# Queueing every weight load from the second paired block on in the order in which its buffer comes free

## The chip, the cores and the metric

The kernel runs on one core of a Trainium2 chip. The metric is the device time of one execution in microseconds; the median of three runs of the kernel before is 1049.4 us (1048.66 to 1050.55). A core has five engines that the text names: PE (TensorE, matrix products), DVE (VectorE), ACT (ScalarE), POOL (GpSimd) and SP (SyncE, which here only issues DMAs). Each has its own list of instructions, in the order in which the kernel wrote them, and they meet through semaphores. In the rows of SP a load whose buffer is not free holds back the loads written behind it.

## What is computed

One layer of a hybrid encoder on 256 rows of width 2048: a differential-attention group and a convolution group side by side, an output projection, then a gated feed-forward network. The part that matters here is the last:

```python
h = h + jnp.einsum('bsm,md->bsd', mixed, w_out[l].astype(mixed.dtype))
hn = rms_norm(h, norm2_g[l])
a = jnp.einsum('bsd,df->bsf', hn, w_gate[l].astype(hn.dtype))
bu = jnp.einsum('bsd,df->bsf', hn, w_up[l].astype(hn.dtype))
h = h + jnp.einsum('bsf,fd->bsd', jax.nn.silu(a) * bu, w_down[l].astype(hn.dtype))
```

w_gate and w_up are 2048 x 5632, w_down is 5632 x 2048, all float32. Every weight is read from device memory once.

## The kernel before

**Products in parts.** A float32 product is made of products in a shorter float format. Each weight tile W is split into a rounded part hi and the rest lo = W - hi, each activation likewise, and PE adds three products: hi by hi, lo activation by hi weight, hi activation by lo weight.

**Chunks.** The program is a list of chunks, each a piece of a weight matrix with its load, its *round* (hi), its *split* (lo) and its *multiply*. There are two kinds.

A *plain* chunk is two slices of 128 rows by 512 columns. `load_chunk` (L305) asks for a buffer `raw`, of which there are `RAW_BUFS` = 5, and has SP load 512 KB into it (L315). `round_chunk` (L318) has ACT make `whi` (L320). For most chunks `split_chunk` (L326) has DVE subtract (L329, `wlo`). For some, marked `by_dma`, ACT writes -raw into `wlo` (L323) and POOL issues a DMA that adds raw to it (L324); this text calls it the accumulate. PE's products are L1014 and L1015 (with hi) and L1020 (with lo). A raw buffer comes free when DVE's split, or the accumulate, has read it.

A *pair* chunk (`kind` "s") takes two slices each of w_gate and w_up (or of two column blocks of w_down) and forms seven combined weights, so that seven products do the work of eight. `load_pair` (L952) has SP load two times 512 KB into a buffer `wb` (L956), of which there are 2; `round_pair` and `split_pair` (L959, L971) use DVE (L966 to L968, L975, L976) and ACT (L969, L972). A pair's buffer comes free with DVE's L975. PE's products are L993 to L995.

**Blocks.** The first 512 columns of the hidden layer (block 0) are plain. Each later block is a paired block: four plain chunks of w_gate, four of w_up and four pairs. The order of its chunks is `FIRST_ORDER` for the first paired block, "gsggsgsuusuu", and `ORDER`, "sggsggsuusuu", for the others (L84, L85). This text writes g1 to g4, u1 to u4 and s1 to s4 for the chunks of the first paired block, and G1, S1 and so on for those of the one after it. Its chunks u2 and u4 are `by_dma`, and so are G1, G2, U2 and U4 of the second. After 4, 4 and 3 blocks comes a pass over w_down of the same two kinds of chunk.

**What sets the order.** `run_chunks` (L387) walks over the chunks. At chunk t it writes down, in this order, splits up to t + 2, pair loads up to t + `PAIR_AHEAD` = t + 6, then for each chunk up to t + 3 its load and its round, more splits, and then the products of chunk t. A pair of the first paired block is not loaded more than three chunks ahead; from the second block on (`behind`, L390) pairs are loaded up to six ahead while plain chunks are loaded three ahead. So a pair's two loads stand in SP's queue ahead of plain loads that are used earlier.

After a block's last product with w_gate, ACT copies a sum out of PE's accumulators (L1092), DVE adds six more (L1094 to L1099), ACT applies SiLU (L1105), and DVE finishes the block (L1113, L1115). These stand on ACT's and DVE's queues between the rounds and splits of the next block's first chunks.

Of the kernel before, what the change touches and what calls it, by code (L numbers as in the profile page):

```python
# [63 lines left out]
RAW_BUFS = 5  # L64
# [14 lines left out]
NS = 4  # L79
# [16 lines left out]

HI_AHEAD, LO_AHEAD = 3, 2

PAIR_AHEAD = 6

FIRSTS = [sum(FGROUPS[: g + 1]) for g in range(len(FGROUPS))]

# [20 lines left out]
def tile_block(  # L123
# [120 lines left out]
    def resume():  # L244
        chunks_done[0] += 1
        for g in list(running):
            if next(g, StopIteration) is StopIteration:
                running.remove(g)
# [14 lines left out]
    side = []  # L263
# [21 lines left out]
    chunks = []  # L285
    before = {}
# [99 lines left out]

    def run_chunks():  # L387
        n = len(chunks)
        i = j = p = 0
        behind = [k for k in range(n) if chunks[k].get("kind") == "s"][NS]  # L390
        for t in range(n):
            hi_lead, lo_lead = lead(t)
            while j < min(i, t + 1 + lo_lead):
                chunks[j]["split"](chunks[j])
                j += 1
            while p < min(n, t + 1 + PAIR_AHEAD):
                if chunks[p].get("kind") == "s":

                    if p < behind and p > t + hi_lead:
                        break  # L400
                    load_pair(chunks[p])
                p += 1
            while i < min(n, t + 1 + hi_lead):
                if i in before:
                    before[i]()
                chunks[i]["load"](chunks[i])
                chunks[i]["round"](chunks[i])
                i += 1
                if hi_lead == lo_lead:
                    chunks[j]["split"](chunks[j])  # L410
                    j += 1
            while j < min(n, t + 1 + lo_lead):
                chunks[j]["split"](chunks[j])
                j += 1
            chunks[t]["multiply"](chunks[t])
            if chunks[t].get("prompt") and chunks[t]["done"]:
                resume()
        while running:
            resume()
# [532 lines left out]
    def load_pair(c):  # L952
        c["b"] = early.tile([P, 4, N], F32, tag="wb", name="wb")
        for i, kind in enumerate("ug"):
            w, col = c["from"][kind]
            sp.dma_start(out=c["b"][:, 2 * i : 2 * i + 2, :],  # L956
                         in_=w.rearrange("(k p) n -> p k n", p=P)[:, c["rows"], col : col + N])
# [82 lines left out]
    def fast_block(order, pairs, twos, sources, operands, half, whole, by_dma=dict(g=(), u=())):  # L1040

        units, sums = [], {}
        left = dict(s=list(pairs), g=list(twos), u=list(twos))
        for kind in order:
            what = left[kind].pop(0)
            c = dict(kind=kind, sums=sums, done=None, first={}, last={}, rows=what["rows"], **operands)
            if kind == "s":
                c.update(p=what["p"], load=lambda c: None, round=round_pair, split=split_pair, multiply=multiply_pair,
                         uses=[q for q, _, _ in PRODUCTS])
                c["from"] = sources  # L1050
            else:
                w, col = sources[kind]
                c.update(ks=what["ks"], w=w, nk=2, width=N, cols=[(col, N)], by_dma=what["k"] in by_dma[kind],
                         load=load_chunk, round=round_chunk, split=split_chunk, multiply=multiply_two,
                         uses=(Q3, QX) if kind == "u" else (Q2, Q4))
            units.append(c)
        assert not any(left.values())
        for q in range(8):
            users = [c for c in units if q in c["uses"]]
            users[0]["first"][q] = users[-1]["last"][q] = True  # L1060
        [c for c in units if c["kind"] != "u"][-1]["done"] = half
        units[-1].update(done=whole, prompt=True)
        chunks.extend(units)

    def gate_up_block(j):
        fast_block(ORDER if j > 1 else FIRST_ORDER, [dict(p=p, rows=slice(p, p + HK + 1, HK)) for p in range(NS)],
                   [dict(ks=ks, rows=slice(ks[0], ks[1] + 1, ks[1] - ks[0]), k=ks) for ks in TWOS],
                   dict(g=(w_gate, j * N), u=(w_up, j * N)),
                   dict(pairs=lambda: forms.get("pair"), plain=lambda k: forms["plain"][k]),
                   products_done, lambda sums: block_done(j, sums),  # L1070
                   BY_DMA if j > 1 and j not in FIRSTS else dict(g=(), u=BY_DMA["u"]))

    def down_pass(g, j0, nb):
        k0 = j0 * HD
        ks = [k for k in range(nb * HD) if k >= 2 * HD or k % HD >= ND]
        twos = [dict(ks=(k0 + a, k0 + b), rows=slice(k0 + a, k0 + b + 1, b - a), k=None)
                for a, b in zip(ks[::2], ks[1::2])]
        for i, order in enumerate(DORDERS[nb]):
            n = 2 * i
            end = {}  # L1080
            fast_block(order, [dict(p=p, rows=slice(k0 + p, k0 + p + HD + 1, HD)) for p in range(ND)], twos,
                       dict(g=(w_down, n * N), u=(w_down, (n + 1) * N)),
                       dict(pairs=lambda: down_forms.get(g), plain=actT.get),
                       lambda sums, n=n, end=end: down_half(g, n, sums, end),
                       lambda sums, n=n, end=end: down_whole(g, n, sums, end))
# [130 lines left out]
    before[OPENING] = lambda: start(late_constants())  # L1216
    before[XWHOLE] = x_whole
    run_chunks()


# [26 lines left out]
```

## Time and profile before

| what | value |
|---|---|
| median of three runs | 1049.4 us |
| profiled execution | 1048.92 us, span 1047.1 us |
| PE busy | 1036.2 us (99%) |
| DVE, ACT, POOL busy | 900.6, 621.6, 100.5 us |
| granted clock | 1.000 |
| loads by SP (queue q1) | 203.71 MB, 56.9% of the 16 DMA engines' span |
| DMAs by POOL (queue q0) | 26.74 MB, 13.4% |

The paired blocks begin at about 383 us of the span. A row of the order of time gives start, duration, engine, line, operation, what it writes and reads, how many it merges, and in brackets how long the engine idled before it and what ended that. SP's rows are the moments of issue; the time from issue to landing stands in the view of DMAs. Names of tiles are the kernel's: raw and wb are the loaded weights, whi and wlo the two parts, wt, wh, wlb and wlt those of a pair, q the accumulators.

### The profile page before, as it was taken

The numbers are of one execution on the slowest core, as the hardware profiler recorded it, in microseconds if no ns is written. First come the engines' busy times: TensorE is split into PE (matmuls) and PEld (weight loads), VectorE is DVE, ScalarE is ACT, GpSimd is POOL, SyncE is SP. The second block draws the span as 40 slices with busy tenths as digits, with TensorE's granted clock in tenths as the row PEclk, the third lists the DMA queues.
The fourth block names the chain that finished last, engine by engine and source line by source line (L and its number), as shares of the span: only waits on it lengthen the run. The fifth ranks groups of instructions, "written<-read, shape, count | busy, mean of one in ns | idle before, by whom it ended". The sixth has DMA issues, their size and how long they took to land.

```text
span 1047.1 us, 12933 instructions
## 1 busy us (share of the span) xinstructions
PE 1036.2 (99%) x4663; PEld 852.5 (81%) x4663; DVE 900.6 (86%) x1095; ACT 621.6 (59%) x786; POOL 100.5 (10%) x143
## 2 busy tenths in 40 slices
PE   9999999999999999999999999999999999999998
PEld 7888887877788788888888888888888888888886
DVE  7899889898765599999787898999878789989897
ACT  7544666755756565776463657666644446657442
POOL 0130122201100100000001010000000110000010
PEclk9999999999999999999999999999999999999999
DMA  9657654453546566987867789879757879798683
GB/s 335 227 182 280 212 163 167 154 181 134 177 153 226 194 223 214 268 266 236 232 210 188 217 271 273 256 217 285 248 175 241 219 208 291 222 287 267 187 265 85
DMA packets 113936, 231.30 MB, mean 221 GB/s; under 512 B 7504, under 2 KB 8656, under 8 KB 113616
## 3 DMA queue, kind: packets, MB, share of 16 engines
q1 hardware_dynamic: 104864, 203.71, 56.9%
q0 software_dynamic: 8864, 26.74, 13.4%
q8 instruction: 36, 0.59, 0.2%
q14 instruction: 28, 0.23, 0.1%
q10 hardware_dynamic: 144, 0.03, 0.0%
HBM read 204.24 MB, written 9.44 MB: 204 GB/s over the span
## 4 chain that ended last, share of the span: by engine, by line
PE 61%; DMA 2%; DVE 2%; issue 1%; ACT 0%; DVEq 0%; POOLq 0%
PE q L1020 12%; PE q L1014 12%; PE q L1015 12%; PE q L995 8%; PE q L993 7%; PE q L994 7%; DMA raw<-in_w_down_dram 1%; PE ps_a L831 1%; DMA wlo<-raw 1%; PE acc L365 1%; PE acc L359 1%; PE acc L360 1%; DVE wlo L329 1%; DVE wlt L976 0%; DVE wt L966 0%
## 5 line engine op out<-in xcount | busy, mean ns | idle before, releaser
L320 ACT CAST whi<-raw 128x1024 fp32r<-128x1024 f32 (+1 forms) x273 | 281.5, 1048 | 141.6 <-PE acc L360 58.9
L329 DVE TENSOR_TENSOR wlo<-raw,whi 128x1024 fp32r<-128x1024 f32 (+1 forms) x239 | 287.8, 1218 | 73.5 <-ACT whi L320 73.3
L972 ACT CAST wh<-wt 128x2048 fp32r<-128x2048 f32 x52 | 99.6, 1914 | 77.6 <-DVE wt L968 76.9
L976 DVE TENSOR_TENSOR wlt<-wt,wh 128x2048 fp32r<-128x2048 f32 x52 | 119.1, 2290 | 14.9 <-ACT wh L972 14.7
L359 PE MATMUL acc<-whi,xhi 128*128 128x512 f32 x320 | 126.9, 397 | 1.0 <-ACT whi L320 0.9
L360 PE MATMUL acc<-whi,xlo 128*128 128x512 f32 x320 | 125.2, 391 | 0.0
L1014 PE MATMUL q<-whi,chi 128*128 128x512 f32 x320 | 125.2, 391 | 0.0
L1015 PE MATMUL q<-whi,clo 128*128 128x512 f32 x320 | 124.5, 389 | 0.0
L993 PE MATMUL q<-wh,fhi 128*128 128x512 f32 x280 | 109.9, 393 | 0.0
L994 PE MATMUL q<-wh,flo 128*128 128x512 f32 x280 | 109.1, 390 | 0.0
L517 DVE SCALAR_TENSOR_TENSOR y<-upad,cw,y 128x256 f32<-128x256 f32 x240 | 102.2, 482 | 2.2 <-ACT y L510 2.2
L1014 PE MATMUL q<-whi,ahi 128*128 128x512 f32 x256 | 100.2, 391 | 0.0
L1015 PE MATMUL q<-whi,alo 128*128 128x512 f32 x256 | 99.6, 389 | 0.0
L975 DVE TENSOR_TENSOR wlb<-wb,wh 128x1536 fp32r<-128x1536 f32 x52 | 91.1, 1752 | 1.8 <-ACT wh L969 1.8
L365 PE MATMUL acc<-wlo,xhi 128*128 128x512 f32 x320 | 87.8, 396 | 2.0 <-DVE wlo L329 2.0
L1020 PE MATMUL q<-wlo,chi 128*128 128x512 f32 x320 | 85.7, 390 | 0.2 <-DMA wlo<-raw 0.2
L969 ACT CAST wh<-wb 128x1536 fp32r<-128x1536 f32 x52 | 76.6, 1474 | 0.0
L365 PEld LDWEIGHTS acc<-wlo,xhi 128*128 128x128 f32 x320 | 59.7, 189 | 15.3 <-DVE wlo L329 3.3
L359 PEld LDWEIGHTS acc<-whi,xhi 128*128 128x128 f32 x320 | 60.4, 189 | 14.3 <-ACT whi L320 1.9
L1020 PEld LDWEIGHTS q<-wlo,chi 128*128 128x128 f32 x320 | 59.9, 188 | 13.2 <-DMA wlo<-raw 0.8
L360 PEld LDWEIGHTS acc<-whi,xlo 128*128 128x128 f32 x320 | 60.4, 189 | 12.2
L1014 PEld LDWEIGHTS q<-whi,chi 128*128 128x128 f32 x320 | 60.1, 188 | 12.3
(230 smaller groups left out, 1739.1 us busy)
## 6 DMA issues: line engine op xcount, KB each, us to landing
raw<-in_w_in_dram SPq DMA_DIRECT2D x79, 512.0 KB, 4.6
raw<-in_w_down_dram SPq DMA_DIRECT2D x64, 512.0 KB, 7.2
raw<-in_w_gate_dram SPq DMA_DIRECT2D x48, 512.0 KB, 7.5
raw<-in_w_up_dram SPq DMA_DIRECT2D x48, 512.0 KB, 6.2
wb<-in_w_up_dram SPq DMA_DIRECT2D x40, 512.0 KB, 3.7
wb<-in_w_gate_dram SPq DMA_DIRECT2D x40, 512.0 KB, 4.9
wlo<-raw POOLq DMA_DIRECT2D x34, 512.0 KB, 7.1
raw<-in_w_out_dram SPq DMA_DIRECT2D x32, 512.0 KB, 4.2
```

The source lines that it names most:

```text
L320: act.copy(c["hi"], c["raw"])
L329: dve.tensor_tensor(c["lo"], c["raw"], c["hi"].bitcast(F32), ALU.subtract)
L359: pe.matmul(ps[m], xhi[:, ms], hi[:, j, :], start=c["first"] and j == 0, stop=False)
L360: pe.matmul(ps[m], xlo[:, ms], hi[:, j, :], start=False, stop=False)
L365: pe.matmul(ps[m], xhi[:, ms], lo[:, j, :], start=False, stop=c["last"] and j == nk - 1)
L517: dve.scalar_tensor_tensor(y[:, ct, :], src, wk, y[:, ct, :], ALU.mult, ALU.add)
L976: dve.tensor_tensor(lot, c["t"], c["hi"][:, :SUMMED].bitcast(F32), ALU.subtract)
L993: pe.matmul(ps, hi, c["hi"][:, w], start=bool(first), stop=False)
L994: pe.matmul(ps, lo, c["hi"][:, w], start=False, stop=False)
L1014: pe.matmul(ps, xs[i][0][:, ms], hi[:, i, :], start=i == 0 and bool(c["first"].get(qs[m])), stop=False)
L1015: pe.matmul(ps, xs[i][1][:, ms], hi[:, i, :], start=False, stop=False)
L1020: pe.matmul(sum_bank(c, qs[m]), xs[i][0][:, ms], lo[:, i, :], start=False, stop=i == 1 and bool(c["last"].get(qs[m])))
```

## The change

`PAIR_AHEAD` goes. From the second paired block on, loads are no longer tied to a distance in chunks. Two lists, `ahead`, hold the plain chunks and the pairs that are not loaded yet, from the second paired block to the end. `freed` says which chunk held the buffer that the head of a list will get (five places back among the plain chunks, two among the pairs), and whether that chunk's split has been written down; for a `by_dma` chunk the walk must have reached it. `load_freed` then queues the loads whose buffer comes free, the earlier chunk's first. It is called twice at each chunk, as soon as the walk is near the first paired block's chunks (`t + hi_lead >= behind - NS`). The first paired block's own loads are still written down when the walk is three chunks away, and a pair's now at the place of its chunk.

```diff
--- before.py
+++ after.py
@@ -96,7 +96,7 @@
 
 HI_AHEAD, LO_AHEAD = 3, 2
 
-PAIR_AHEAD = 6
+PAIR_BUFS = 2
 
 FIRSTS = [sum(FGROUPS[: g + 1]) for g in range(len(FGROUPS))]
 
@@ -386,32 +386,62 @@
 
     def run_chunks():
         n = len(chunks)
-        i = j = p = 0
-        behind = [k for k in range(n) if chunks[k].get("kind") == "s"][NS]
+        i = j = 0
+        pairs = [k for k in range(n) if chunks[k].get("kind") == "s"]
+        raws = [k for k in range(n) if chunks[k].get("kind") != "s" and not chunks[k].get("spare_raw")]
+        behind = pairs[NS]
+        loaded, split = set(), set()
+
+        def load(k):
+            if k not in loaded:
+                loaded.add(k)
+                if k in before:
+                    before[k]()
+                chunks[k]["load" if chunks[k].get("kind") != "s" else "fetch"](chunks[k])
+
+        def split_next():
+            chunks[j]["split"](chunks[j])
+            split.add(j)
+
+        ahead = [[which[a] for a in range(len(which)) if which[a] >= behind] for which in (raws, pairs)]
+        place = [{k: a for a, k in enumerate(which)} for which in (raws, pairs)]
+
+        def freed(side, t):
+
+            if not ahead[side]:
+                return None
+            k = (raws, pairs)[side][place[side][ahead[side][0]] - (RAW_BUFS, PAIR_BUFS)[side]]
+            return k if k in split and (t >= k or not chunks[k]["by_dma"]) else None
+
+        def load_freed(t):
+            while True:
+                ready = [(k, side) for side in range(2) if (k := freed(side, t)) is not None]
+                if not ready:
+                    return
+                load(ahead[min(ready)[1]].pop(0))
+
         for t in range(n):
             hi_lead, lo_lead = lead(t)
             while j < min(i, t + 1 + lo_lead):
-                chunks[j]["split"](chunks[j])
+                split_next()
                 j += 1
-            while p < min(n, t + 1 + PAIR_AHEAD):
-                if chunks[p].get("kind") == "s":
-
-                    if p < behind and p > t + hi_lead:
-                        break
-                    load_pair(chunks[p])
-                p += 1
+            if t + hi_lead >= behind - NS:
+                load_freed(t)
             while i < min(n, t + 1 + hi_lead):
-                if i in before:
-                    before[i]()
-                chunks[i]["load"](chunks[i])
+                load(i)
+                for which in ahead:
+                    if i in which:
+                        which.remove(i)
                 chunks[i]["round"](chunks[i])
                 i += 1
                 if hi_lead == lo_lead:
-                    chunks[j]["split"](chunks[j])
+                    split_next()
                     j += 1
             while j < min(n, t + 1 + lo_lead):
-                chunks[j]["split"](chunks[j])
+                split_next()
                 j += 1
+            if t + hi_lead >= behind - NS:
+                load_freed(t)
             chunks[t]["multiply"](chunks[t])
             if chunks[t].get("prompt") and chunks[t]["done"]:
                 resume()
@@ -1045,7 +1075,7 @@
             what = left[kind].pop(0)
             c = dict(kind=kind, sums=sums, done=None, first={}, last={}, rows=what["rows"], **operands)
             if kind == "s":
-                c.update(p=what["p"], load=lambda c: None, round=round_pair, split=split_pair, multiply=multiply_pair,
+                c.update(p=what["p"], fetch=load_pair, by_dma=False, round=round_pair, split=split_pair, multiply=multiply_pair,
                          uses=[q for q, _, _ in PRODUCTS])
                 c["from"] = sources
             else:
```

The instructions of PE, DVE, ACT and POOL stand in the same order before and after. Only SP's queue changes. The first place is the joint between the first and the second paired block, on SP, before. wb_3906 is s4, wb_3909 S1 and wb_3982 S2 (each in two loads); raw_3859, raw_3887, raw_3944 and raw_3963 are u1 to u4, raw_4017 and raw_4049 G1 and G2. What a row waits for stands in brackets by engine or DMA counter.

```order
L315 DMA raw_3859<-in_w_up_dram 128x2x512 [waits DMAHW7_49]
L315 DMA raw_3887<-in_w_up_dram 128x2x512 [waits DMAHW0_49]
L956 DMA wb_3906<-in_w_up_dram 128x2x512 [waits DMAHW2_49,DMAHW3_49,DMAHW1_49,DVE_49]
L956 DMA wb_3906<-in_w_gate_dram 128x2x512
L956 DMA wb_3909<-in_w_up_dram 128x2x512 [waits DMAHW6_49,DMAHW5_49,DVE_49]
L956 DMA wb_3909<-in_w_gate_dram 128x2x512 [waits DMAHW4_49]
L315 DMA raw_3944<-in_w_up_dram 128x2x512
L315 DMA raw_3963<-in_w_up_dram 128x2x512
L956 DMA wb_3982<-in_w_up_dram 128x2x512 [waits DMAHW2_49,DMAHW7_49,DMAHW1_49,DVE_49]
L956 DMA wb_3982<-in_w_gate_dram 128x2x512 [waits DMAHW0_49]
L315 DMA raw_4017<-in_w_gate_dram 128x2x512
L315 DMA raw_4049<-in_w_gate_dram 128x2x512
```

The same place after. wb_3889 is S1, wb_3913 s4, wb_3948 S2; raw_3892 is G2, raw_3894 u2, raw_3951 u3, raw_3970 and raw_3972 G3 and G4, raw_3974 u4. G1 (raw_3887) stands just ahead of the first row.

```order
L986 DMA wb_3889<-in_w_up_dram 128x2x512 [waits DMAHW2_49,DMAHW3_49,DMAHW1_49,DVE_49]
L986 DMA wb_3889<-in_w_gate_dram 128x2x512
L315 DMA raw_3892<-in_w_gate_dram 128x2x512
L315 DMA raw_3894<-in_w_up_dram 128x2x512 [waits DMAHW4_49]
L986 DMA wb_3913<-in_w_up_dram 128x2x512 [waits DMAHW6_49,DMAHW5_49,DVE_49]
L986 DMA wb_3913<-in_w_gate_dram 128x2x512
L986 DMA wb_3948<-in_w_up_dram 128x2x512 [waits DMAHW6_49,DMAHW7_49,DMAHW5_49,DVE_49]
L986 DMA wb_3948<-in_w_gate_dram 128x2x512 [waits DMAHW0_49]
L315 DMA raw_3951<-in_w_up_dram 128x2x512 [waits DMAHW1_49]
L315 DMA raw_3970<-in_w_gate_dram 128x2x512 [waits DMAHW2_49]
L315 DMA raw_3972<-in_w_gate_dram 128x2x512 [waits DMAHW4_49,DMAHW3_49,DMASW0_49]
L315 DMA raw_3974<-in_w_up_dram 128x2x512 [waits DMAHW1_49,DVE_49]
```

S1 has moved ahead of s4, S2 ahead of u3, and G1 to G4 ahead of u4; u4's load now waits for DVE.

On ACT nothing moved. This is its order at the same place after, which the steps of the prediction follow: u3, u4 with the accumulate's first half, S1, G1, the sums of the first paired block, G2.

```order
L320 CAST whi_3953<-raw_3951 128x1024 [waits DMAHW1_49,PE_49,Activation_49]
L320 CAST whi_3976<-raw_3974 128x1024 [waits DMAHW4_49,PE_49,Activation_49]
L323 ACTIVATE wlo_3978<-raw_3974 128x1024 [waits PE_49]
L999 CAST wh_3994<-wb_3889 128x1536 [waits DMAHW2_49]
L1002 CAST wh_3994<-wt_3993 128x2048 [waits DVE_49]
L320 CAST whi_4028<-raw_3887 128x1024 [waits DMAHW0_49,PE_49,Activation_49]
L323 ACTIVATE wlo_4030<-raw_3887 128x1024 [waits DMASW0_49,PE_49]
L1122 COPY sum0_4041<-q0_3791 128x512 [waits PE_49]
L1135 ACTIVATE sum0_4041<-sum0_4041 128x512 [waits DVE_49]
L1135 ACTIVATE sum2_4043<-sum2_4043 128x512 [waits DVE_49]
L320 CAST whi_4060<-raw_3892 128x1024 [waits DMAHW3_49,PE_49,Activation_49]
L323 ACTIVATE wlo_4062<-raw_3892 128x1024 [waits PE_49]
```

The rows show that everything of the next block on ACT stands behind u3's and u4's rounds.

The second place is a later block (the second of the second group), on SP, before. wb_5613 is its pair S2, wb_5703 S3; the raw rows are G1 to G4.

```order
L956 DMA wb_5613<-in_w_up_dram 128x2x512 [waits DMAHW7_49,DMAHW0_49,DVE_49]
L956 DMA wb_5613<-in_w_gate_dram 128x2x512
L315 DMA raw_5648<-in_w_gate_dram 128x2x512 [waits DMAHW1_49]
L315 DMA raw_5680<-in_w_gate_dram 128x2x512 [waits DMAHW2_49]
L956 DMA wb_5703<-in_w_up_dram 128x2x512 [waits DMAHW4_49,DMAHW3_49,DVE_49]
L956 DMA wb_5703<-in_w_gate_dram 128x2x512
L315 DMA raw_5752<-in_w_gate_dram 128x2x512 [waits DMAHW5_49,DMASW2_49]
L315 DMA raw_5770<-in_w_gate_dram 128x2x512 [waits DMAHW6_49]
```

The same block after; wb_5513 is S1 and wb_5583 S2.

```order
L315 DMA raw_5479<-in_w_gate_dram 128x2x512 [waits DMAHW5_49,DVE_49]
L986 DMA wb_5513<-in_w_up_dram 128x2x512 [waits DMAHW7_49,DMAHW6_49,DVE_49]
L986 DMA wb_5513<-in_w_gate_dram 128x2x512
L315 DMA raw_5532<-in_w_gate_dram 128x2x512 [waits DMAHW0_49,DVE_49]
L986 DMA wb_5583<-in_w_up_dram 128x2x512 [waits DMAHW2_49,DMAHW3_49,DMAHW1_49,DVE_49]
L986 DMA wb_5583<-in_w_gate_dram 128x2x512
L315 DMA raw_5603<-in_w_gate_dram 128x2x512 [waits DMASW2_49]
L315 DMA raw_5605<-in_w_gate_dram 128x2x512 [waits DMAHW4_49,DVE_49]
```

The pairs no longer run ahead: G1 now stands before S1 and G2 before S2, where before S2 stood ahead of both.

## The prediction

> **What bounds the kernel now.** I read the shares of the engines first, then tables of windows, then who waits for whom, and last the order of time around the joint of the first two paired blocks. The page:
>
> ```profile
> PE 1036.2 (99%) x4663; PEld 852.5 (81%) x4663; DVE 900.6 (86%) x1095; ACT 621.6 (59%) x786; POOL 100.5 (10%) x143
> ```
>
> TensorE is the bound. The change acts from 383 us on, where the paired blocks begin, so the table of windows is cut there (columns: window, its length, PE busy with its matmuls, granted clock, share of the DMA engines, GB/s):
>
> ```profile
> 383.00:1005.00 622.00, 621.60 (x2780) 1.00 0.79 238
> 1005.00:1047.10 42.10, 37.87 (x165) 1.00 0.60 174
> ```
>
> In 622 us PE idles 0.4 us; in the last 42 us it idles 4.2, most of it the output's tail. So no order of loads can win more than 4.6 us, and hardly more than 0.6. The clock is full throughout.
>
> [...]
>
> The waits from 383 us on (who waited, for whom: total us, times, longest):
>
> ```profile
> SPq L956 <- DVE wlb L975: 336.4, 41, 13.4
> SPq L315 <- DVE wlo L329: 131.0, 49, 11.2
> ACT whi L320 <- DMA raw<-in_w_down_dram: 22.7, 5, 7.7
> PE q L1020 <- DMA wlo<-raw: 0.2, 1, 0.2
> ```
>
> SP's queue of loads really stands behind pair loads (L956) that wait for a buffer, and ScalarE does wait for plain loads behind them. But PE, which uses a chunk three chunks after it is loaded, lost 0.2 us by it. The waits that the change can remove are covered already. What it can add has no such cover, so I looked for loads that are queued later.
>
> **The change, part by part.** PE, DVE, ACT and POOL keep their order; SP has the same loads in another one. No instruction is added to the four; where the new order of issue needs more separate waits on SP, they stand in front of loads that would wait anyway, so I cost them at nothing.
>
> *In the second and later paired blocks* plain loads go ahead of the pair loads that were queued up to six chunks early. The nearest price of what this frees is the 22.7 us of ACT above, which lay under PE's work: 0 to 0.6 us gained, and I take 0.2.
>
> *At the joint of the first and second paired block* the order shows three loads of the first block put behind loads of the second: pair s4 behind S1; plain u3 behind S2; plain u4 behind G3 and G4. u4 also gets no buffer of its own: of the five, G1, G2, G3 and G4 (all used after u4) hold four and u3 the fifth, so its wait on DVE is one for the split of u3. This is SP before (x2 is two loads):
>
> ```profile
> 402.15 0.37 SPq L956 DMA_DIRECT2D wb<-in_w_up_dram  x1
> 410.15 0.37 SPq L956 DMA_DIRECT2D wb<-in_w_up_dram  x1
> 410.56 0.47 SPq L956 DMA_DIRECT2D wb<-in_w_gate_dram  x1
> 411.07 0.98 SPq L315 DMA_DIRECT2D raw<-in_w_up_dram  x2
> 418.74 0.37 SPq L956 DMA_DIRECT2D wb<-in_w_up_dram  x1
> 419.75 0.98 SPq L315 DMA_DIRECT2D raw<-in_w_gate_dram  x2
> ```
>
> 402.15 is s4, 410.15 S1, 411.07 u3 and u4, 418.74 S2, each pair load the moment its buffer is split. Times from issue to landing, in this order: the second half of the pair at 410.56; the plain load at 411.07; a plain load behind a pair with no accumulate running (393.03, and the shortest, 853.13); two plain loads alone (978 to 985); the accumulates (wlo<-raw) from 383 to 980, min/median/max; the one issued at 436.97.
>
> ```profile
> wb<-in_w_gate_dram SPq DMA_DIRECT2D x1, 512.0 KB, 4.5
> raw<-in_w_up_dram SPq DMA_DIRECT2D x1, 512.0 KB, 7.4
> raw<-in_w_up_dram SPq DMA_DIRECT2D x1, 512.0 KB, 6.1
> raw<-in_w_gate_dram SPq DMA_DIRECT2D x1, 512.0 KB, 5.4
> raw<-in_w_down_dram SPq DMA_DIRECT2D x2, 512.0 KB, 3.5
> DMA to landing us min/median/max: 5.0/7.1/10.2
> DMA to landing us min/median/max: 5.6/5.6/5.6
> ```
>
> The engines that use these loads, before, VectorE first, then ScalarE, POOL and PE:
>
> ```profile
> 414.38 1.22 DVE L966 TENSOR_TENSOR wt<-wb 128x1024 f32<-128x1024 f32 x1
> 416.96 1.75 DVE L975 TENSOR_TENSOR wlb<-wb,wh 128x1536 fp32r<-128x1536 f32 x1
> 421.23 1.22 DVE L329 TENSOR_TENSOR wlo<-raw,whi 128x1024 fp32r<-128x1024 f32 x1
> ```
>
> ```profile
> 418.90 2.09 ACT L320 CAST whi<-raw 128x1024 fp32r<-128x1024 f32 x2
> 420.89 1.05 ACT L323 ACTIVATE wlo<-raw 128x1024 fp32r<-128x1024 f32 x1
> 421.85 1.46 ACT L969 CAST wh<-wb 128x1536 fp32r<-128x1536 f32 x1
> 425.07 1.91 ACT L972 CAST wh<-wt 128x2048 fp32r<-128x2048 f32 x1 [1.76 <-DVE wt L968]
> 427.42 1.05 ACT L320 CAST whi<-raw 128x1024 fp32r<-128x1024 f32 x1 [0.43 <-DMA raw<-in_w_gate_dram]
> 429.34 0.56 ACT L1092 COPY sum<-q 128x512 f32<-128x512 f32 x1
> 433.45 1.23 ACT L1105 ACTIVATE sum<-sum 128x512 f32<-128x512 f32 x2 [3.54 <-DVE sum L1098]
> 435.52 1.06 ACT L323 ACTIVATE wlo<-raw 128x1024 fp32r<-128x1024 f32 x1
> ```
>
> ```profile
> 422.25 0.87 POOL L324 DMA_DIRECT2D wlo<-raw  x1 [7.75 <-ACT wlo L323]
> 436.97 0.87 POOL L324 DMA_DIRECT2D wlo<-raw  x1 [6.39 <-ACT wlo L323]
> ```
>
> ```profile
> 422.36 1.20 PE L1020 MATMUL q<-wlo,chi 128*128 128x512 f32 x4 [0.25 <-DMA wlo<-raw]
> 432.69 1.07 PE L1020 MATMUL q<-wlo,chi 128*128 128x512 f32 x4
> 443.39 1.07 PE L1020 MATMUL q<-wlo,chi 128*128 128x512 f32 x4
> ```
>
> 418.90 rounds u3 and u4, 420.89 with POOL's 422.25 is u4's accumulate, for PE's products at 432.69; 427.42 is G1, 435.52 with 436.97 is G2, for PE's at 443.39. Now step by step:
>
> 1. s4 takes the place of S1: issued at 410.15, second half landed 410.56 + 4.5 = 415.06. DVE began it at 414.38, so 0.7 late; its split L975 ends 416.96 + 1.75 + 0.7 = 419.4.
> 2. S2's loads wait for that split, and u3's load behind them. From the pair's issue to the plain load is 419.75 - 418.74 = 1.0, so u3 is issued at 420.4 instead of 411.07. Its landing: 5.4 to 7.4; I take 6.1, since u2's accumulate, with two loads fewer beside it than before, is done by then. Landed 426.5.
> 3. ACT rounds u3 (1.05), DVE splits it (1.22): 428.8.
> 4. u4 is issued then and lands 3.5 later, with nothing ahead of it: 432.3.
> 5. ACT's L320 and L323 for it take 2.0 (0.95 from start to start, then 1.05): 434.3. POOL begins 0.3 after L323 (420.89 + 1.05 to 422.25) at 434.6; the accumulate takes 5.0 to 10.2, and I take the 5.6 of the one with least beside it: 440.2. PE wanted it at 432.69: **7.5 us late**.
> 6. Behind u4's L323 (start 433.3) ACT still has S1's casts, G1 and the copy L1092: L969 at 434.3, L972 at 435.6 (its wt is ready, DVE took it up at 428.8 and its three steps, which span 414.38 to about 417, take 2.6), L320 at 437.4, L323 at 438.4, L1092 at 439.4. Before, L1092 stood at 429.34: 10.0 late.
> 7. From L1092 through DVE's sums to L1105, G2's L323 and POOL at 436.97 is one chain, so POOL issues G2's accumulate at 447.0; with 5.6 it lands at 452.6. PE's products at 443.39 then come **9.2 us late**, which contains the 7.5. Behind that DVE and ACT are 10 us behind the old times and PE 9.2, and later chunks get their loads early; I add nothing.
>
> PE, 99% busy, cannot win lost time back. Sum: 9.2 - 0.2 = +9.0. The profiled execution took 1048.92 (span 1047.1 and 1.8 around it), 0.5 under the median of the runs, 1049.4; on the median that is **1058.4**. Lower end of the likeliest case: landing 5.4, accumulate 5.0, gain 0.6: +7.3, 1056.7. Upper: landing 7.4 and an accumulate of 10.2 instead of 5.6: 9.2 + 1.3 + 4.6 = +15.1, 1064.5.
>
> **The rivals.** *Faster.* ACT's waits for loads vanish and the joint costs nothing. For it: the 22.7 us. Against it: the 4.6 us of idle PE; even all of it would give 1044.8. It decides only if u4's accumulate lands by 432.69, for which u3 would have to be issued 7.5 us before 420.4, at 412.9, and S2's wait, which ended at 418.74 before, stands ahead of it. Chance 0.03.
>
> *No change.* The joint's delay is hidden, or loads are reissued in time. Same condition, and 1049.2. For it: three chunks of lead. Against it: the order. Chance 0.05.
>
> *Much slower: accumulates lose in every block.* More loads in flight could lengthen every accumulate:
>
> ```profile
> 687.19 0.88 POOL L324 DMA_DIRECT2D wlo<-raw  x1 [6.28 <-DVE sum L1115]
> 694.99 0.39 PE L1020 MATMUL q<-wlo,chi 128*128 128x512 f32 x1
> ```
>
> This one, a block's G2 again, has 7.8 us from issue to use; at the longest time, 10.2, PE would wait 2.4. Five later blocks have one such: 12 us, so 1058.4 + 12 = 1070. Against it: the bytes are the same, and clumps of four loads behind a pair are broken up. Chance 0.09. [...]
>
> *Slower by less, 1050.5 to 1054.* If ACT or DVE recover some steps by order of time I cannot see. Chance 0.08.
>
> **How the numbers follow.** The likeliest case (the joint's delay, 1056.7 to 1064.5) has 0.75. The range 1054 to 1065 holds it and a little of the smaller loss; outside lie the other three. A change under 0.2% (2.1 us) cannot be told from none with this kernel. Faster 0.03, same 0.06 (no change and the faintest losses), slower 0.91.
>
> **What would show it.** PE waits of some 9 us for DMA wlo<-raw between 430 and 455 us, in about two pieces, and PE full again after; SP issuing a plain load of w_up near 420 and another near 429; ACT waiting near 420 to 432 for raw<-in_w_up_dram; ACT's 22.7 us for w_down gone. Wrong if u3's load is issued before S2's, or if PE's lost time is spread over the later blocks.

## The result, and the profile after

The kernel after takes 1058.38 us (median of five runs, 1057.63 to 1059.61), the kernel before 1049.17 (five runs, 1048.66 to 1050.55). The ratio is 1.0088, with a 95% interval of 1.0073 to 1.0102: 9.2 us slower. The forecast was 1058.4. The profiled execution of after took 1057.63 us, with a span of 1055.9.

From the page after, its first line:

```profile
PE 1037.9 (98%) x4663; PEld 853.6 (81%) x4663; DVE 900.8 (85%) x1095; ACT 622.2 (59%) x786; POOL 100.4 (10%) x143
```

The table of windows after, cut as before, and then with the joint by itself (window, length, PE busy with its matmuls, PEld, DVE, ACT, POOL, granted clock, DMA share, GB/s):

```profile
383.00:1005.00 622.00, 615.49 (x2739) 507.18 (x2738) 541.85 (x528) 364.38 (x338) 43.40 (x50) 0.99 0.80 235
1005.00:1055.90 50.90, 46.58 (x204) 37.54 (x202) 41.55 (x45) 19.52 (x17) 5.71 (x8) 1.00 0.57 165
...
425.00:460.00 35.00, 28.64 (x117) 22.78 (x116) 27.95 (x30) 22.26 (x22) 2.59 (x3) 0.90 0.77 221
460.00:1005.00 545.00, 545.00 (x2438) 450.39 (x2437) 477.13 (x468) 320.87 (x300) 39.88 (x46) 1.00 0.81 237
```

The same 35 us at the joint in the kernel before:

```profile
425.00:460.00 35.00, 35.00 (x160) 28.97 (x159) 32.58 (x34) 24.53 (x24) 2.59 (x3) 1.00 0.84 241
```

All of the loss lies there: 117 products started where there were 160, and 43 products of 35/160 = 0.219 us are 9.4 us. From 460 us on PE is full. But only 6.4 us of the 9.2 are idle; the clock of 0.90 holds the rest. The waits of PE from 383 us on, and ScalarE's for loads:

```profile
PE q L1050 <- DMA wlo<-raw: 3.8, 1, 3.8
PE q L1044 <- ACT whi L320: 2.6, 1, 2.6
...
ACT whi L320 <- DMA raw<-in_w_up_dram: 11.0, 2, 6.2
ACT whi L320 <- DMA raw<-in_w_down_dram: 2.4, 1, 2.4
```

ScalarE's 22.7 us of waits for w_down are down to 2.4, as the change meant, and 11.0 us for w_up at the joint stand in their place. The order of time there, after (lines behind the diff are 30 higher than before: L956 is L986, L966 L996, L975 L1005, L1014 L1044, L1020 L1050, L1092 L1122). SP: s4's first load, S2's, u3, G3 and G4, u4.

```profile
409.72 0.37 SPq L986 DMA_DIRECT2D wb<-in_w_up_dram  x1
...
419.21 0.37 SPq L986 DMA_DIRECT2D wb<-in_w_up_dram  x1
...
420.13 0.47 SPq L315 DMA_DIRECT2D raw<-in_w_up_dram  x1
420.65 1.09 SPq L315 DMA_DIRECT2D raw<-in_w_gate_dram  x2
427.97 0.37 SPq L315 DMA_DIRECT2D raw<-in_w_up_dram  x1
```

VectorE (s4, then u3's split), ScalarE (u3, u4 with its accumulate's first half, S1, the copy of the sums, the SiLU, G2's first half) and POOL (u4's accumulate, G2's):

```profile
414.83 1.23 DVE L996 TENSOR_TENSOR wt<-wb 128x1024 f32<-128x1024 f32 x1 [0.80 <-DMA wb<-in_w_gate_dram]
417.43 1.75 DVE L1005 TENSOR_TENSOR wlb<-wb,wh 128x1536 fp32r<-128x1536 f32 x1
426.72 1.23 DVE L329 TENSOR_TENSOR wlo<-raw,whi 128x1024 fp32r<-128x1024 f32 x1 [4.93 <-ACT whi L320]
```

```profile
425.63 1.05 ACT L320 CAST whi<-raw 128x1024 fp32r<-128x1024 f32 x1 [6.17 <-DMA raw<-in_w_up_dram]
431.53 1.04 ACT L320 CAST whi<-raw 128x1024 fp32r<-128x1024 f32 x1 [4.85 <-DMA raw<-in_w_up_dram]
432.48 1.06 ACT L323 ACTIVATE wlo<-raw 128x1024 fp32r<-128x1024 f32 x1
...
438.51 0.56 ACT L1122 COPY sum<-q 128x512 f32<-128x512 f32 x1
442.62 1.23 ACT L1135 ACTIVATE sum<-sum 128x512 f32<-128x512 f32 x2 [3.54 <-DVE sum L1128]
...
444.70 1.06 ACT L323 ACTIVATE wlo<-raw 128x1024 fp32r<-128x1024 f32 x1
```

```profile
433.85 0.87 POOL L324 DMA_DIRECT2D wlo<-raw  x1 [19.77 <-ACT wlo L323]
...
446.16 0.87 POOL L324 DMA_DIRECT2D wlo<-raw  x1 [6.40 <-ACT wlo L323]
```

And PE: u4's products with the rounded half, u4's with its accumulate, G2's with its accumulate.

```profile
432.63 0.50 PE L1044 MATMUL q<-whi,chi 128*128 128x512 f32 x1 [2.57 <-ACT whi L320]
...
438.53 2.07 PE L1050 MATMUL q<-wlo,chi 128*128 128x512 f32 x4 [3.79 <-DMA wlo<-raw]
...
452.18 1.07 PE L1050 MATMUL q<-wlo,chi 128*128 128x512 f32 x4
```

The chain stands as forecast up to 438.5. Then comes something that no step had: the four products at 438.53 take 2.07 us in place of 1.07. Three windows of 3.41 us from 434.38 on show why:

```profile
434.38:437.79 3.41, 0.36 (x2) 0.00 (x0) 2.81 (x2) 3.41 (x4) 0.33 (x1) 1.00 0.83 154
437.79:441.20 3.41, 2.67 (x6) 2.15 (x7) 3.12 (x4) 1.29 (x2) 0.86 (x1) 0.50 1.04 323
441.20:444.62 3.42, 3.42 (x9) 2.64 (x8) 3.42 (x7) 2.00 (x3) 0.00 (x0) 0.50 0.98 226
```

While PE waited, its granted clock fell to one half, and stayed there for 6.83 us. Fourteen products started 0.427 us apart instead of 0.227: 2.8 us, which with the 6.4 idle makes 9.2. And G2's products, where step 7 had PE wait for G2's accumulate (issued at 446.16, 5.7 us to landing, so 451.9), started at 452.18 without a wait. Was the half clock a second loss beside the forecast's chain, or did it only fill the time in which PE would have waited for G2's accumulate? That, and whether the single steps carry what the forecast gave them, is what the experiments ask. Differences to before below are those to the runs of before taken beside the kernel.

### The profile page after: what moved, and what is told of

The parts are those of the page before. It is cut to its first block, busy times and chain, and to the rows that moved or that the text cites. A ratio compares the mean times of both kernels' runs of the same rounds, so it can differ in the third digit from the quotient of the medians.

```text
span 1055.9 us, 12966 instructions
## 1 busy us (share of the span) xinstructions
PE 1037.9 (98%) x4663; PEld 853.6 (81%) x4663; DVE 900.8 (85%) x1095; ACT 622.2 (59%) x786; POOL 100.4 (10%) x143
## 4 chain that ended last, share of the span: by engine, by line
PE 59%; DVE 3%; DMA 2%; issue 1%; ACT 1%; SPq 0%; DVEq 0%; POOLq 0%; ACTq 0%
PE q L1050 11%; PE q L1044 11%; PE q L1045 11%; PE q L1025 7%; PE q L1023 7%; PE q L1024 7%; DVE wlo L329 1%; DMA raw<-in_w_up_dram 1%; PE ps_a L861 1%; PE acc L365 1%; PE acc L359 1%; PE acc L360 1%; DVE wt L996 1%; DVE wlb L1005 1%; DMA wlo<-raw 0%
## 5 line engine op out<-in xcount | busy, mean ns | idle before, releaser
L1044 PE MATMUL q<-whi,chi 128*128 128x512 f32 x320 | 125.3, 392 | 2.6 <-ACT whi L320 2.6
L1044 PE MATMUL q<-whi,ahi 128*128 128x512 f32 x256 | 100.2, 391 | 0.0
L1005 DVE TENSOR_TENSOR wlb<-wb,wh 128x1536 fp32r<-128x1536 f32 x52 | 91.1, 1752 | 5.6 <-ACT wh L999 5.6
L1050 PE MATMUL q<-wlo,chi 128*128 128x512 f32 x320 | 86.5, 393 | 3.8 <-DMA wlo<-raw 3.8
L1050 PEld LDWEIGHTS q<-wlo,chi 128*128 128x128 f32 x320 | 60.5, 189 | 16.7 <-DMA wlo<-raw 4.2
L1044 PEld LDWEIGHTS q<-whi,chi 128*128 128x128 f32 x320 | 60.1, 188 | 15.3 <-ACT whi L320 3.0
L1045 PEld LDWEIGHTS q<-whi,clo 128*128 128x128 f32 x320 | 60.1, 188 | 12.2
```

The costliest lines, as they stand in the source:

```text
L1044: pe.matmul(ps, xs[i][0][:, ms], hi[:, i, :], start=i == 0 and bool(c["first"].get(qs[m])), stop=False)
L1045: pe.matmul(ps, xs[i][1][:, ms], hi[:, i, :], start=False, stop=False)
L1050: pe.matmul(sum_bank(c, qs[m]), xs[i][0][:, ms], lo[:, i, :], start=False, stop=i == 1 and bool(c["last"].get(qs[m])))
```

## The experiments

### Is the whole loss at the joint?

The rule starts only when all chunks of the first paired block are loaded; the later blocks are queued as after.

```diff
-            if t + hi_lead >= behind - NS:
+            if i >= behind:
                 load_freed(t)
```

(at both places)

> The new order starts only when the walk has loaded all chunks of the first paired block, so the joint of the first and second paired block is queued as before and every later block as after. The theory that the joint holds the whole loss: TensorE waits nowhere for more than 0.5 us between 383 and 1005 us, its clock stays at 1.00, ScalarE's 22.7 us of waits for w_down are down to a few, and the time is 1048.6 to 1049.4, the 0.2 us gain that the prediction took included. The rival that later blocks cost too (longer accumulates, as in the much slower case): waits of TensorE for wlo<-raw near 550, 690 or 850 us and a time over 1051.

The joint is not quite queued as before, as this expectation has it: S1 and S2 no longer run ahead either, and all loads of the first paired block go out ahead of those of the second: u3 and u4 at 402.91, where before had 411.07.

It took 1048.46 us (11 runs) beside 1048.34 of before (15 runs): ratio 1.0000, 0.9991 to 1.0008. PE is full and at full clock:

```profile
425.00:460.00 35.00, 35.00 (x160) 28.98 (x159) 33.15 (x33) 25.00 (x25) 2.59 (x3) 1.00 0.96 270
460.00:1005.00 545.00, 545.00 (x2438) 450.18 (x2437) 476.50 (x467) 318.73 (x297) 39.02 (x45) 1.00 0.81 237
```

No wait of ScalarE for a load is left in this trace; all of the 22.7 us are gone, and nothing is gained. So the joint holds the whole loss, and the new order of the later blocks is worth nothing, to within the 0.9 us of the interval. The forecast's gain of 0.2 us is too small to be told in it, and none was seen.

### Steps 2 and 4, one at a time

Step 2 alone, in the old kernel: S2's two loads written ahead of u3's and u4's.

```diff
-            while p < min(n, t + 1 + PAIR_AHEAD):
+            while p < min(n, t + 1 + PAIR_AHEAD + (2 if t in (behind - 5, behind - 4) else 0)):
```

> The old kernel with one exchange: S2's two loads are written ahead of u3's and u4's; everything else, u4's own buffer too, stands as before. If step 2's order alone makes a loss, SP issues u3 near 419.7 instead of 411, u4 0.5 later, u4's accumulate lands near 435, TensorE waits some 3 us there and some 2 us for G2's, and the time is 1053 to 1055, as in the run that gave u4 its buffer back (1054.5). If that run's loss came from other parts of the new order (S1 ahead of s4, the later blocks), this one stays under 1050.5.

1052.47 us beside 1048.52: ratio 1.0038 (1.0023 to 1.0053), 4.0 us. SP's u3 and u4, and where PE waited:

```profile
419.44 0.98 SPq L315 DMA_DIRECT2D raw<-in_w_up_dram  x2
```

```profile
433.26 1.20 PE L1020 MATMUL q<-wlo,chi 128*128 128x512 f32 x4 [1.18 <-DMA wlo<-raw]
437.74 0.50 PE L993 MATMUL q<-wh,fhi 128*128 128x512 f32 x1 [1.02 <-DVE sum L1098]
```

One exchange in SP's order costs 4 us in a kernel that is otherwise the old one. The time is half a microsecond under the expected range; the accumulate landed at 433.2, not 435, and G2's cost hardly a wait. The second wait is new: the fourth product of S1, the next block's first pair, wants one of PE's accumulators (q) that VectorE (L1098) has not yet read, because the sums, behind u4's round on ScalarE, are late.

Step 4 without step 2: S2 waits until u3 is queued, the rest as after. Step 1 stays in: S1 still goes out ahead of s4.

```diff
-            if not ahead[side]:
+            if not ahead[side] or (side == 1 and ahead[1][0] != behind and behind - 2 not in loaded):
                 return None
```

> As after, but S2's loads wait until u3's are queued, so step 2 is undone and step 4 left: u3 goes out near 411, u4 still stands behind G3 and G4 and waits for u3's split. By the steps u4 goes out near 422.5 and lands near 429, its accumulate lands near 436.6 (a wait of some 4 us), G2's near 449.6 (2 more): 6 to 7 us over before, 1054 to 1056. So each of steps 2 and 4 would cost about 6 alone, and both together 10. If the two add up, step 4 costs what the run without it gave back, 4 us, and the time is 1052 to 1052.6.

1054.68 us beside 1048.52: ratio 1.0060 (1.0045 to 1.0075), 6.2 us, as the steps said. u3 and u4 on SP, and the two waits of PE:

```profile
410.64 0.47 SPq L315 DMA_DIRECT2D raw<-in_w_up_dram  x1
...
423.09 0.37 SPq L315 DMA_DIRECT2D raw<-in_w_up_dram  x1
```

```profile
435.41 1.19 PE L1050 MATMUL q<-wlo,chi 128*128 128x512 f32 x4 [3.54 <-DMA wlo<-raw]
448.73 1.19 PE L1050 MATMUL q<-wlo,chi 128*128 128x512 f32 x4 [0.74 <-DMA wlo<-raw]
```

Here G2's accumulate is the next wait, as step 7 has it.

Step 4 undone, step 2 left: plain loads of the second block wait for the first block's.

```diff
-            if not ahead[side]:
+            if not ahead[side] or (side == 0 and i < behind):
                 return None
```

> As after, but the plain loads of the second paired block wait their turn until the first paired block's are queued; pairs stay as after, so u3 still stands behind S2. u4 then gets its own buffer again and is issued 0.5 us behind u3. If step 4 (u4 waits for u3's split, because G1 to G4 hold the buffers) is most of the loss: u4 lands near 427, its accumulate near 434.5, TensorE waits 2 to 3 us there and up to 1.5 for G2's, no half clock, time 1051 to 1053. If it is step 2 (u3 behind S2) that makes most of the loss, the time stays at 1056 or more.

1054.47 us beside 1048.34: ratio 1.0064 (1.0050 to 1.0077), 6.1 us, between what the two theories gave. Both steps count: 4.0 us for step 2 alone, 6.1 for step 2 with step 1, 6.2 for step 4 with step 1, and, further down, 1.0 for step 1 alone and 10.0 for all. Whether they overlap is open. Both delay the same load, u4; but 4.0 and 6.2 add up to 10.2, as if there were no overlap, while 6.1 and 6.2 less the 1.0 that is in both make 11.3. With intervals of some 1.5 us either way the runs do not decide it.

### The half clock, and step 7

Products that add nothing keep PE busy in its two waits: 27 of them, 11 ahead of u4's products and 16 between its halves. Their weights are all zero, and nothing of the computation changes.

```diff
+        def nothing(n):
+            if c["done"] and c["by_dma"] and c["ks"][0] == 14 and not spent:
+                for _ in range(n):
+                    pe.matmul(sum_bank(c, qs[0]), zero, forms["pair"][0][0].rearrange("p a b -> p (a b)"), start=False, stop=False)
...
+            nothing(11)
             for i in range(2):
                 for m in range(NM):
                     first_half(m)
             resume()
+            nothing(16)
             for m in range(NM):
                 second_half(m)
```

> As after, with 27 products with all-zero weights added (they add zero to a sum that is open): 11 in TensorE's wait for u4's rounded half and 16 in its wait for u4's accumulate, 0.22 us each, so that TensorE is hardly idle there. Nothing else is changed. If the half clock of 438 to 445 us comes from TensorE's idling, the clock stays at 1.00. Then there are two theories of what follows. That the half clock's 2.8 us stand on the path alone: 1058.4 - 2.8 = 1055.6. That step 7 holds, and TensorE, 2.8 us earlier, waits for G2's accumulate (landed at 451.8) instead: 1058.1, with a wait for wlo<-raw of some 2.4 us near 449 to 452. If the clock falls all the same, idling is not its cause, and the time is 1058.4.

And with 0 and 5 of them:

> As the kernel with zero products, but with none in the first wait and 5 at the start of the second, which leaves 2.6 us idle there and about 2.7 us idle before the accumulate lands, instead of 2.6 and 3.8. If one unbroken idle time of more than about 3 us is what halves the clock, it stays at 1.00 and the time is that of the kernel with 27 zero products. If idle time is summed over a longer stretch, the clock falls, and the time stays at 1058.4.

The first took 1060.61 us (1059.25 to 1062.24; ratio 1.0112, 1.0097 to 1.0128), the second 1058.13 (ratio 1.0093, 1.0079 to 1.0107). The kernel after was also run and profiled once more, beside the kernel of the next section:

> The kernel after, unchanged, on the same chip and beside the same runs of before as the next one: 1.0088 of before, 9.2 us.

1058.42 beside 1048.45: ratio 1.0100 (1.0085 to 1.0114). G2's products in these three traces, in this order (L1054 is L1050 of the first two kernels):

```profile
454.02 1.57 PE L1054 MATMUL q<-wlo,chi 128*128 128x512 f32 x4 [2.00 <-DMA wlo<-raw]
```

```profile
452.74 1.20 PE L1054 MATMUL q<-wlo,chi 128*128 128x512 f32 x4 [1.15 <-DMA wlo<-raw]
```

```profile
452.77 1.20 PE L1050 MATMUL q<-wlo,chi 128*128 128x512 f32 x4 [0.99 <-DMA wlo<-raw]
```

With 27 products PE waited 0.57 us for u4's rounded half and not at all for its accumulate, and the clock stayed at 1.00 until PE had come to G2's products, so idling was the cause of its fall at the joint. But PE then waited 2.0 us for G2's accumulate, and in two runs whose clock was 1.000 as a whole, the time was 1059.25 and 1059.42, not 1055.6. In the other two traces the clock fell (0.90 from 425 to 460 us in both), but in other places than in the first trace of after (for the 5 products even in the first wait, of 3.06 us, so their own question, whether 2.7 us idle is short enough, was not put), and PE waited for G2's accumulate as well. So a half clock ahead of G2's products is no loss of its own here; step 7's accumulate sets the end. Behind them it is one: the other two runs with 27 products had a clock of 0.998 and took 1061.81 and 1062.24 us, and in the traced one, the slower, the clock was at one half from 454.63 to 458.05, after the wait for G2. By that trace it is half of 3.4 us, 1.7, of the difference of 2.4 to 3.0. That the kernel with 27 products is 1 us slower than after even at full clock is not explained in full. Beside the second trace of after, which is from the same chip, L1122 starts 0.6 us later in its trace (439.76, where it is line L1135, for 439.18) and G2's accumulate takes 0.7 longer (6.6 for 5.9); why, no run shows.

Last, step 5 against step 7: u4 is split by VectorE, so that no accumulate of u4 is waited for.

```diff
-                   BY_DMA if j > 1 and j not in FIRSTS else dict(g=(), u=BY_DMA["u"]))
+                   BY_DMA if j > 1 and j not in FIRSTS else dict(g=(), u=BY_DMA["u"][: 1 if j == 1 else None]))
```

> As after, but u4 is split by VectorE and not by the accumulate, so step 5's wait goes: TensorE finds u4's low half at 433.8, before it wants it. Step 7 says that G2's accumulate sets the end by a chain of its own: ScalarE comes to G2 only 1 us earlier, it lands at 451 to 452, TensorE waits 5 to 6 us there instead, and the time is 1056.5, up to 1059.5 if the clock falls to one half there with nothing behind it that hides it. If step 5's wait (3.8) and the half clock behind it (2.8) are the loss themselves, the time is 1051.8.

1059.43 us beside 1048.52: ratio 1.0105 (1.0088 to 1.0122). The wait of 3.8 us is gone and the time is no better. But PE didn't wait where step 7 put it. ScalarE and PE:

```profile
436.51 1.91 ACT L1002 CAST wh<-wt 128x2048 fp32r<-128x2048 f32 x1 [2.50 <-DVE wt L998]
...
440.22 0.56 ACT L1122 COPY sum<-q 128x512 f32<-128x512 f32 x1
```

```profile
440.84 0.79 PE L1023 MATMUL q<-wh,fhi 128*128 128x512 f32 x1 [3.56 <-ACT sum L1122]
```

VectorE's added split puts off S1's steps, and with them the copy L1122, and PE's next block needs the accumulator (q) which that copy reads. So the chain through the block's sums, step 6, reaches PE here by an accumulator and not by G2's accumulate. A half clock came on top (rows 0.43 us apart from 441.43 to 446.55): 14 products at 0.43 us in place of 0.23 are 2.8 us. Only a part of it counts. G2's accumulate landed at 452.2 (issued at 447.75, 4.5 to landing) and PE took it at 453.53; at full clock PE would have come to it at about 450.7, as an estimate from these rows, and have waited after all. So some 1.3 of the 10.9 us are the clock's. The rival's 1051.8 is out.

The chain itself is the same in every trace. Where L1122 starts, when POOL issues G2's accumulate, when PE takes it, all from the traces, and the time over before, from the medians:

| kernel | L1122 | G2 issued | G2 taken | over before, us |
|---|---|---|---|---|
| before | 429.34 | 436.97 | 443.39 | 0 |
| rule from the second block on | 428.65 | 436.29 | 442.63 | 0.1 |
| step 2 alone | 433.61 | 441.25 | 445.80 | 4.0 |
| steps 1 and 4 | 435.41 | 443.06 | 448.73 | 6.2 |
| after | 438.51 | 446.16 | 452.18 | 9.2 |
| after, again | 439.18 | 446.82 | 452.77 | 10.0 |
| u4 split by VectorE | 440.22 | 447.75 | 453.53 | 10.9 |

From L1122 to the issue are 7.5 to 7.7 us in each row, and in the traces that are not in the table too. Below the first two rows, whose times are equal within the interval, the times stand in the order in which L1122 starts and G2 is taken. Trace against trace it is closer: by how much later than in before (443.39) PE takes G2's accumulate is how much longer the span is, to 0.6 us in each row (8.8 and 8.8 us for after). The span is longer by more only where something is lost behind G2, as in the trace with 27 products (10.6 and 13.1).

### Step 1: s4 behind S1

Step 1 undone: pairs of the second block wait until s4 is queued. It ran twice, the second time beside after.

```diff
-            if not ahead[side]:
+            if not ahead[side] or (side == 1 and not loaded.issuperset(pairs[:NS])):
                 return None
```

> As after, but pairs of the second block wait until s4 is queued: s4 goes out at 402 again and S1 at 410. Step 1 says that S2 and u3 behind it then go out 0.7 to 0.9 us earlier, and all that follows with them: 0.7 to 0.9 us under after, 1.0080 of before in place of 1.0088. If s4's place doesn't count, because u3 and u4 wait for transfers and not for s4's split, the ratio stays at 1.0088.

> The kernel with s4 queued ahead of S1 once more, now beside the kernel after on one chip. If step 1 is worth its 0.7 us, it is 0.7 to 0.9 us faster than after; if u4's load and the two accumulates take back what u3 wins, 0 to 0.4 us.

The first time 1057.95 us, ratio 1.0091 (1.0076 to 1.0106); the second time 1057.01 (five runs, 1056.79 to 1058.19), ratio 1.0082 (1.0068 to 1.0097), beside 1058.42 of after. That is 1.4 us between medians on one chip. The intervals of the ratios overlap, but each of the five runs is below each of the four of after. The traces of the two show the step itself: without it S2 goes out at 418.67 and not 419.64, and L1122 starts at 438.33 and not 439.18. So step 1 is worth some 0.9 us by the chain, where 0.7 was said; whether it is the 1.4 of the medians is open, and the first pair of runs does not show it.

Step 1 alone, with steps 2 and 4 undone:

```diff
-            if not ahead[side]:
+            if not ahead[side] or (i < behind if side == 0 else ahead[1][0] != behind and behind - 1 not in loaded):
                 return None
```

> As after, with steps 2 and 4 both undone and step 1 left: S1 still goes out ahead of s4, but u3 and u4 are queued ahead of S2 and of G1 to G4, so both go out near 411 to 412. If steps 2 and 4 are the whole loss, TensorE's waits at the joint stay under 0.5 us, the clock at 1.00, and the time is that of before within 0.6 us. If s4's later place, or the later blocks, hold a part of the loss, it shows here alone: 1 us or more over before.

1049.46 us (11 runs) beside 1048.45: ratio 1.0011 (1.0001 to 1.0020), 1.0 us, within the noise that the forecast named, but not zero. Its trace is of the slowest of the 11 runs, 1050.87, and shows two waits of PE, 2.0 us together, in places that step 1 does not speak of: one for u2's accumulate and one for an accumulate in a pass over w_down:

```profile
423.26 0.96 PE L1050 MATMUL q<-wlo,chi 128*128 128x512 f32 x3 [1.17 <-DMA wlo<-raw]
...
518.11 1.20 PE L1050 MATMUL q<-wlo,chi 128*128 128x512 f32 x4 [0.88 <-DMA wlo<-raw]
```

The first took 8.7 us from issue to landing in before and 9.7 here, with G1's load at 412.09 beside it; the second, issued at 506.76, took 11.3, where before's at 505.90 took 6.7. By the medians 9.0 of the 10.0 us go with steps 2 and 4. Where the last microsecond of the other runs lies, at G1's load, in the later blocks or at s4, this one trace does not show.

None of these versions beats the kernel before.

## Why the prediction was right

The time came out as worked, and most of its steps too. That it did so to 0.1 us is luck: the difference to before was 9.0 in the forecast, 9.2 here and 10.0 when the same kernel was run again. Trace times of after are 0.4 us earlier than before's up to the joint (409.72 for 410.15), so 0.4 is to be added when they are held against the steps.

- *Step 1*: L1005 ended at 419.2 (419.4 said). Right, and worth some 0.9 us by the chain.
- *Step 2*: u3 issued at 420.13 (420.4), rounded from 425.63 on (landing 426.5 said). Right; alone it is worth 4.0 us.
- *Steps 3 and 4*: u3's split ended at 427.95 (428.8), u4 was issued at 427.97 and rounded from 431.53 on, 3.56 later (3.5 said). Right, and worth 6.2 us together with step 1.
- *Step 5*: mis-sized by 1 us. The accumulate took 4.6 us, not 5.6, so PE was late by 6.4 us and not by 7.5; the lower end of the range had 5.0 for it. And not all of the 6.4 was a wait for the accumulate: PE first stood 2.6 us for u4's rounded half, which the step doesn't name, then 3.8 for the accumulate.
- *Step 6*: L1122 at 438.51 (439.4). Right, and what the next block waits for is more than the step said: it reads the accumulators that PE needs, and in five of the traces PE waited 0.5 to 3.6 us for these sums.
- *Step 7*: G2's accumulate landed at 451.9 (452.6). Right as the mechanism that sets the end; but in the first trace the half clock filled the wait. The forecast had the clock at full throughout and named no cost for idling. It came out right without it only because the lost 2.8 us lay under a wait that was coming anyway (PE took G2's accumulate 0.3 us after it landed), and that is luck. Where nothing covers it, as in the two slower runs with 27 products and in part with u4 split by VectorE, it adds.
- *Later blocks*: 0.2 us of gain was forecast, none was seen. ScalarE's 22.7 us were covered to the last.
- *The signs*: the two late loads of w_up (420.13 and 427.97), ScalarE's 11.0 us of waits for them, the 22.7 us down to 2.4 and a full PE behind the joint were all seen. The 9 us of waits for wlo<-raw in two pieces were not: PE waited so for 3.8 us in the first trace and 3.5 in the second; the rest was u4's rounded half and the half clock.

Of the rivals, the accumulates that lose in every block are out: in the trace of after PE is full from 460 us on, and with the rule from the second block on the ratio is 1.0000. Single ones do lose: in four of the twelve traces with a changed order PE waits for an accumulate between 460 and 1005 us, 0.4 to 0.9 us at a time, and the longest took 11.3 us, where before's longest was 10.2. The smaller loss did not come, since no engine recovered a step: ScalarE was 9.2 us behind before at L1122, and POOL 9.2 at G2's issue.

## What to carry to other kernels

A queue that is sorted by when buffers come free is not sorted by when the data is wanted; at a seam where two stages share buffers and one queue, find the last loads of the old stage in the new order and follow each one to its consumer. Behind a late load look for the in-order engine that everything of the next stage has to pass: the copy of the old stage's sums stood there, and it set the end, not the wait that looked largest. Take out that wait alone and the time may not move.

## What the hardware showed beside this

In nine traces the granted clock fell in mid-program, twelve times in all, and each time to one half. It stayed there for 3.4 us (3.41 with step 4 undone, 3.42 with 27 products) or for twice that (6.83 in the first trace of after), and it fell at other times from run to run of the same kernel (once in the first trace of after, at 437.79; twice in the second, near 432.8 and 439.6 by PE's rows). Two stretches of the kernel with step 4 undone (the clock stayed at 1.00 after the first and was at 0.50 after the second), and the one of the kernel with 27 products after which its clock fell:

```profile
433.86:437.28 3.42, 1.74 (x8) 1.44 (x9) 3.21 (x3) 1.87 (x3) 0.86 (x1) 1.00 1.01 326
447.51:450.93 3.42, 1.27 (x5) 1.05 (x6) 3.42 (x3) 2.54 (x3) 0.00 (x0) 1.00 1.03 334
```

```profile
451.22:454.63 3.41, 1.41 (x7) 0.87 (x6) 3.23 (x2) 3.41 (x4) 0.00 (x0) 1.00 0.97 290
```

In the first of the three PE was idle for 1.68 us, and the clock stayed; in the other two for 2.15 and 2.00 us, and it fell. In the 3.4 us ahead of each of the twelve falls PE was idle for 2.0 to 3.1 us. No run asks what lies between 1.68 and 2.00 us, or what sets the moment of a fall. How long the half clock lasted differs too: 6.83 us in the first trace of after, where PE was still idle for 0.74 of the first 3.41, and 3.4 after the first fall of the second, where it was idle for some 0.5. So the stall of 3.79 us in after went with 6.83 us at half speed, and the one of 2.00 us with 27 products with 3.42.
